# Two transformer blocks on one core: fillers that set the place of TensorE's operands in the on-chip memory

## The chip, the cores and the metric

One core of a Trainium2 chip. The metric is the device time of one execution in microseconds, the median of several runs.

## The reference

Two blocks of one layer each follow each other on 256 tokens of width 1024, with 16 learned tokens in front, all in fp32. The first mixes with two convolutions and then picks 16 of 16384 experts per token and head; the second has two kinds of attention, gates, and a feed-forward part.

```python
def first_block(x, meta_tokens, ...):
    ...
        proj = hn @ w_in[l]
    ...
        y = jnp.concatenate([rms_norm(y_sc, out_norm_g_sc[l]), rms_norm(y_cf, out_norm_g_cf[l])], axis=-1)
        h = h + y @ w_out[l]
        hn = rms_norm(h, norm_ffn_g[l])
        h = h + peer_layer(hn, peer_w_q[l], peer_sub_keys[l], peer_u[l], peer_v[l])
...
def second_block(x, meta, ...):
    ...
        proj = xn @ w_in[l]
        sb_q, sb_k, sb_v, df_q, df_k, df_v = jnp.split(proj, splits, axis=-1)
    ...
        y_sb = o_sb @ w_br_sb[l]
        y_df = o_df @ w_br_df[l]
        gates = jax.nn.sigmoid(xn @ w_gate[l] + b_gate[l]).reshape(B, L_pad, 2, D)
        merged = gates[:, :, 0] * y_sb + gates[:, :, 1] * y_df
        h = h + merged @ w_out[l]
        hn = rmsnorm(h, norm_ffn_g[l])
        h = h + (jax.nn.silu(hn @ w_ffn_gate[l]) * (hn @ w_ffn_up[l])) @ w_ffn_down[l]
    y = rmsnorm(h, norm_final_g)
    return y[:, N_META:N_META + S]
```

All 128 x 128 experts are computed for all tokens (`u`, then `v`), and the 16 chosen ones of each head get their gates.

## The kernel before, in words

**Units.** All large weights are cut into 454 units of 128 x 1024, listed in the order of use. SyncE's queue loads a unit into `raw` (five buffers, `load_to`); ScalarE copies it, rounded to fp32r, to `hi`, and VectorE writes the rest, `raw - hi`, to `lo` (three buffers each, `split_to`, lines 152 and 154). An activation is split in the same way. A product is three matmuls, hi x hi, hi x lo and lo x hi, summed in PSUM.

**Two kinds of matmul.** `mm_w` (lines 183 to 185) takes a unit as the stationary operand: for each of eight chunks of 128 columns it sends 256 or 272 columns of the activation through, 24 matmuls a unit. `mm_a` (lines 197 to 199) takes the activation as the stationary operand, 128 columns for each half of the tokens, and sends 512 columns of the unit through, 12 matmuls a unit. Each matmul loads its own 128 columns of weights; the profile calls those loads PEld, and they lie beside the matmul ahead.

**Stages, in order.** The projections of the first block from `xT` (`gg`, `ga`, `cg`, `xv`, `bg`); its output `wo` (`mm_a`, from `yhi`, `ylo`); queries `q` and 128 expert units `u` from `hThi`, `hTlo`; between these the routing, and in the second half of `u` the gate products `gp` (128-column fp32 matmuls in `pair`, taken from the list `pend` in the middle of a unit or ahead of one); 128 expert outputs `v` (`mm_a`, from `w_hi`, `w_lo`); six projections of the second block from `xT2` with the attention's own small matmuls between them (`stick`, `diff`); the gates `g`; the branches `ysb` and `ydf` from `osb` and `odf`; `o` (`mm_a`, from `mghi`, `mglo`); then `fg` and `fu` from `hThi`, `hTlo` and, in two halves within each `fg` unit, `fd` (`mm_a`, from `f_hi`, `f_lo`).

**Order.** TensorE's and SyncE's orders are as written; a scheduler orders the other engines. POOL's queue saves `h` (`hsave`, line 511), and loads it back with two gain rows towards the end of `v` (lines 835 to 840).

**Places.** A tile is a stretch of bytes that begins at the same place in each of the 128 partitions. A pool lays its tiles one behind the other, rounded up to 32 bytes, and pools stand on each other as a stack: 16384 bytes of scratch for the descriptors that POOL writes, then `const` (in it `hThi` and `hTlo`), `wraw`, `whi`, `wlo`, and the pools of the phases (`pc`, `pa`, `pb`, `pq`, `psb`, `pm`, `pf`). So every tile's place depends on all that stand ahead of it. In the attention, `sq` and `dq` (queries) and `sv` and `dv` (values) have two buffers each.

Of the kernel before, what the change touches and what calls it, by code (L numbers as in the profile page):

```python
# [9 lines left out]
F32 = mybir.dt.float32  # L10
# [9 lines left out]
P = 128  # L20
# [15 lines left out]
XN = 2  # L36
WARM = 9
SOON = 60

_VECS = [  # L40
    ("norm_mix_g", 8), ("norm_mix_g_2", 8), ("b_gate_2", 16),
# [11 lines left out]
def two_blocks(ctx, tc, x, feats, vecs, w_in, w_out, w_q, keys, u, v, final_g, meta2, w_in2, lams, w_gate,  # L53
               w_br_sb, w_br_df, w_out2, w_fg, w_fu, w_fd, final_g2, gains, out):
    nc = tc.nc
# [9 lines left out]
    def phase(name):  # L65
        st = ExitStack()
        pool = st.enter_context(tc.tile_pool(name=name, bufs=1, reuse_waits="tile"))
        return st, pool

    def mm_tile(name):  # L70
        return pmm.tile([P, 512], F32, tag="mm", name=name)
# [226 lines left out]
    s_c, pc = phase("pc")  # L298
# [160 lines left out]

    gf = gain_row(pc, 1, "gf", nc.sync)  # L460
    h = xt
    for br, (y, gname) in enumerate(((ysc, "out_norm_g_sc"), (cf, "out_norm_g_cf"))):
        ysq = pc.tile([P, 4, T], F32, tag=f"ysq{br}", name=f"ysq{br}")
        yhi = pc.tile([P, 4, T], F32R, tag=f"yhi{br}", name=f"yhi{br}")
        ylo = pc.tile([P, 4, T], F32R, tag=f"ylo{br}", name=f"ylo{br}")
        with first():
            for c in range(4):
                nc.scalar.activation(yhi[:, c, :], y[:, c, :], AF.Copy, scale=col(gname, c))
                nc.vector.scalar_tensor_tensor(ylo[:, c, :], y[:, c, :], col(gname, c), yhi[:, c, :].bitcast(F32),
                                               op0=ALU.mult, op1=ALU.subtract)  # L470
            for c in range(4):
                nc.scalar.activation(ysq[:, c, :], y[:, c, :], AF.Square)
            fold(ysq, 4, nc.gpsimd)
        acc = [mm_tile(f"wo{i}") for i in range(4)] if br == 0 else acc_tiles("wo1_")
        for c in range(4):
            if c < 2:
                mm_a(acc, [(yhi[:, c], ylo[:, c])], c == 0, False)
            elif c == 3:
                mm_a(acc, [(yhi[:, 2], ylo[:, 2]), (yhi[:, 3], ylo[:, 3])], False, True)
            if br == 0 and c == 0:  # L480
                with first():
                    norm_mean()
            if br == 0 and c == 1:
                with first():
                    norm_var()
            if c == 1:
                pss = at_tile(f"pss{br}") if br == 0 else mm_tile(f"pss{br}")
                for t in range(2):
                    nc.tensor.matmul(pss[:, t:t + 1], ysq[:, 0, t * P:(t + 1) * P], ones[:, :1], start=True, stop=True)
                rs = pc.tile([P, 2], F32, tag=f"rsb{br}", name=f"rsb{br}")  # L490
                nc.scalar.activation(rs, pss[:, :2], AF.Sqrt, bias=eps, scale=1.0 / 512)
                nc.vector.reciprocal(rs, rs)
        with first():
            for t in range(2):
                for b in range(2):
                    bs = slice(b * 512, (b + 1) * 512)
                    nc.vector.scalar_tensor_tensor(h[t][:, bs], acc[2 * t + b], rs[:, t:t + 1],
                                                   h[t][:, bs], op0=ALU.mult, op1=ALU.add)
# [29 lines left out]
    nc.sync.dma_start(lm, lams.broadcast_to((P, 4, 64)))  # L528
    lam = const.tile([P, 1], F32, tag="lam", name="lam")
    sg8 = const.tile([P, 1], F32, tag="sg8", name="sg8")  # L530

    vals_a = pr.tile([P, 2, NH, TOPK], F32, tag="vals", name="vals")
    pos_a = pr.tile([P, 2, NH, TOPK], U32, tag="pos", name="pos")
# [308 lines left out]
    s_q, pq = phase("pq")  # L842
# [5 lines left out]
    with first():  # L848
# [7 lines left out]
        for t in range(2):  # L856
            s1s.append(sq_sum(pb, hts[t], P, f"r2_{t}", junk))
    rsb = pq.tile([P, L], F32, tag="rsb", name="rsb")
    nc.gpsimd.memset(rsb[:, :NM], 1.0)

    def x2_norm():
# [87 lines left out]
    def stick(hd, q, k, vT):  # L949
        pz = at_tile(f"z{hd}")  # L950
        for kt in range(3):
            nc.tensor.matmul(pz[:, qcols(kt)], k[:, kt * P:(kt + 1) * P], q[:, Q0[kt]:], start=True, stop=True)
        z = psb.tile([P, NQ], F32, tag="z", name=f"zs{hd}", bufs=2)
        nc.vector.tensor_tensor(z, pz[:, :NQ], mneg, op=ALU.add)
        e = psb.tile([P, NQ], F32, tag="e", name=f"e{hd}", bufs=2)
        nc.scalar.activation(e, z, AF.Abs)
        nc.scalar.activation(e, e, AF.Exp, scale=-1.0)
        nc.scalar.activation(e, e, AF.Ln, bias=1.0)
        nc.vector.scalar_tensor_tensor(e, z, 0.0, e, op0=ALU.max, op1=ALU.add)
        yield  # L960
        vt = value(f"sv{hd}", "sv", vT)
        yield
        yield
        ps = at_tile(f"S{hd}")
        for kt in range(3):
            for j in range(kt, 3):
                nc.tensor.matmul(ps[:, qcols(kt, j)], tri if j == kt else ones, e[:, qcols(j)],
                                 start=(j == kt), stop=(j == 2))
        nc.vector.tensor_tensor(z, z, ps[:, :NQ], op=ALU.subtract)
        nc.scalar.activation(z, z, AF.Exp)  # L970
        yield
        yield
        po = at_tile(f"po{hd}")
        for kt in range(3):
            nc.tensor.matmul(po[:, Q0[kt]:T], vt[:, kt, :], z[:, qcols(kt)], start=(kt == 0), stop=(kt == 2))
        nc.scalar.activation(osb[0][:, hd, :], po[:, :T], AF.Copy)
        nc.vector.tensor_tensor(osb[1][:, hd, :], po[:, :T], osb[0][:, hd, :].bitcast(F32), op=ALU.subtract)
# [3 lines left out]
    def diff(hd, q, k, vT):  # L981
        slope = 2.0 ** (-(hd + 1))
        ws = []
        for t in range(2):
            kn = KN[t]
            nm = psb.tile([P, 2], F32, tag="nm", name=f"nm{hd}{t}", bufs=2)
            sm = psb.tile([P, 2], F32, tag="dsm", name=f"dsm{hd}{t}", bufs=2)
            pe = []
            for c in range(2):
                cs = slice(64 * c, 64 * c + 64)  # L990
                ps = at_tile(f"ds{hd}{t}{c}")
                nc.tensor.matmul(ps[:, :kn], q[cs, t * P:(t + 1) * P], k[cs, :kn], start=True, stop=True)
                s = psb.tile([P, kn], F32, tag=f"ds{t}{c}", name=f"dss{hd}{t}{c}", bufs=2)
                nc.vector.scalar_tensor_tensor(s, dist[t], -slope, ps[:, :kn], op0=ALU.mult, op1=ALU.add)
                nc.vector.tensor_reduce(nm[:, c:c + 1], s, axis=AX.X, op=ALU.max, negate=True)
                nc.scalar.activation(s, s, AF.Exp, bias=nm[:, c:c + 1], accum_out=sm[:, c:c + 1])
                pe.append(s)
            nc.vector.reciprocal(sm, sm)
            nc.vector.tensor_scalar(pe[1], pe[1], sm[:, 1:2], lam, op0=ALU.mult, op1=ALU.mult)
            w = padded[f"w{t}"][0]  # L1000
            nc.vector.scalar_tensor_tensor(w[:, :kn], pe[0], sm[:, 0:1], pe[1], op0=ALU.mult, op1=ALU.subtract)
            ws.append(w)
            if t == 0:
                yield
        vt = value(f"dv{hd}", "dv", vT)
        yield
        yield
        outs = []
        for t in range(2):
            nk = KW[t] // P  # L1010
            pw = at_tile(f"pw{hd}{t}")
            wT = psb.tile([P, 3, P], F32, tag="wT", name=f"wT{hd}{t}", bufs=2)
            for i in range(nk):
                nc.tensor.transpose(pw[:, i * P:(i + 1) * P], ws[t][:, i * P:(i + 1) * P], ident)
            nc.scalar.activation(wT[:, :nk, :], pw[:, :KW[t]].rearrange("p (a b) -> p a b", a=nk), AF.Copy)
            outs.append(wT)
        yield
        for t, wT in enumerate(outs):
            nk = KW[t] // P
            po = at_tile(f"dpo{hd}{t}")  # L1020
            for i in range(nk):
                nc.tensor.matmul(po[:, :P], wT[:, i, :], vt[:, i, :], start=(i == 0), stop=(i == nk - 1))
            nc.scalar.activation(od[t][:, hd, :], po[:, :P], AF.Copy)
# [25 lines left out]
                running.remove(g)  # L1049

    for hd in range(NH):
        q = feat(f"sq{hd}", hd, "sq", QS, float(P) ** -0.5) if hd != 1 else ahead
        if hd > 1:
            q = q()
            advance()
# [9 lines left out]
                cols = x2_norm()  # L1065
        vT = feat(f"svT{hd}", hd, "vT", FULL)
        if hd == 0:
            ahead = feat("sq1", 1, "sq", QS, float(P) ** -0.5)
            with first():
                across(pb, cols, rsb[:, QS], "rsb")  # L1070
            tc.keep_in_program_order(nc.scalar.preload_act_table_set("natural_log_exp_and_others"))
            q, k = q(), k()
# [4 lines left out]
            with queued([latest["hi"], latest["lo"]]):  # L1077
                small_parts()
    for hd in range(NH):
        q = feat(f"dq{hd}", hd, "dq", QS, 0.125)()  # L1080
        advance()
        k = feat(f"dk{hd}", hd, "k", FULL)()
        advance()
# [49 lines left out]
    nc.gpsimd.dma_start(gb2, final_g2.broadcast_to((P, D)))  # L1133
    acc = acc_tiles("fd")
    rsf = pf_.tile([P, T], F32, tag="rsf", name="rsf")
    prev = []

    def swish(m, pg, pu):
# [116 lines left out]
```

## Time and profile before

| | us |
|---|---|
| median of 3 runs (lowest, highest) | 1455.7 (1454.81, 1459.09) |
| the profiled execution | 1458.83 |
| its span, first to last instruction | 1456.8 |
| TensorE busy with matmuls | 1437.5 |
| VectorE, ScalarE, POOL busy | 1049.4, 741.1, 14.5 |
| TensorE's share of the chain that ended last | 92% |

The span lies within the profiled execution's own time. A line of the profile names the engine, the line of the kernel, the operation, output and inputs; PE is TensorE, DVE VectorE, ACT ScalarE. A matmul's record begins when it starts, and its end is modelled: records overlap, and the distance from start to start tells how fast they follow each other.

### The profile page before, as it was taken

Reading aid. Unit: us, or ns where it says so; the run is one execution under the profiler, and the core shown is the slowest. Engines: PE = TensorE matmul, PEld = TensorE weight load, DVE = VectorE, ACT = ScalarE, POOL = GpSimd, SP = SyncE. Lnnn points to the kernel's source line nnn. Section 1 sums busy time; section 2 is a strip of 40 time slices with the busy share of each in tenths; the row PEclk is TensorE's granted clock in tenths of the full one; section 3 lists DMA queues with packets and bytes.
Section 4 is the critical chain, followed back from the end, with each engine's and each line's share of the span. In section 5 each row is a group of like instructions: output and inputs, shape, how many; then the busy total and the mean of one; then the engine's idle time right before and its main releaser. Section 6 shows DMA issues by size and latency. Waiting matters only on the chain.

```text
span 1456.8 us, 25628 instructions
## 1 busy us (share of the span) xinstructions
PE 1437.5 (99%) x10114; PEld 1339.5 (92%) x10114; DVE 1049.4 (72%) x1887; ACT 741.1 (51%) x1236; POOL 14.5 (1%) x35
## 2 busy tenths in 40 slices
PE   8999999999999999999999999999999999999998
PEld 8988999999999999888888888899999999899997
DVE  8997789885889999655555565665577766766666
ACT  7555544544444444544444544564455764544444
POOL 0010000000000000000000000100000000000000
PEclk9999999999999999999999999999999999999999
DMA  7525565666444444566666676554344466555563
GB/s 242 198 73 186 194 186 174 192 198 194 145 138 138 145 146 137 181 191 198 190 192 197 191 247 197 175 172 127 121 130 125 137 178 186 172 179 184 188 191 100
DMA packets 69816, 248.96 MB, mean 171 GB/s; under 512 B 7744, under 2 KB 9152, under 8 KB 69696
## 3 DMA queue, kind: packets, MB, share of 16 engines
q1 hardware_dynamic: 68256, 242.61, 53.4%
q0 software_dynamic: 1152, 4.19, 0.8%
q8 instruction: 79, 1.29, 0.4%
q10 hardware_dynamic: 288, 0.52, 0.1%
q14 instruction: 41, 0.34, 0.1%
HBM read 245.20 MB, written 2.10 MB: 170 GB/s over the span
## 4 chain that ended last, share of the span: by engine, by line
PE 92%; DVE 6%; issue 1%; ACT 0%; DMA 0%; SPq 0%; DVEq 0%; ACTq 0%
PE v L197 8%; PE v L199 8%; PE v L198 8%; PE u L185 7%; PE u L183 7%; PE u L184 7%; PE gp L712 4%; DVE lo L154 2%; PE fg L184 1%; PE fg L185 1%; PE fu L185 1%; PE fu L183 1%; PE fu L184 1%; PE fg L183 1%; PE fd L199 1%; PE fd L198 1%
## 5 line engine op out<-in xcount | busy, mean ns | idle before, releaser
L154 DVE TENSOR_TENSOR lo<-raw,hi 128x1024 fp32r<-128x1024 f32 x453 | 551.4, 1222 | 233.2 <-ACT hi L152 231.4
L152 ACT ACTIVATE hi<-raw 128x1024 fp32r<-128x1024 f32 x453 | 476.3, 1057 | 406.8 <-PE u L184 98.2
L183 PE MATMUL u<-hThi,hi 128*128 128x256 f32 x1024 | 292.6, 286 | 0.0
L185 PE MATMUL u<-hThi,lo 128*128 128x256 f32 x1024 | 285.0, 278 | 0.9 <-DVE lo L154 0.6
L184 PE MATMUL u<-hTlo,hi 128*128 128x256 f32 x1024 | 284.5, 278 | 0.0
L198 PE MATMUL v<-lo,w_hi 128*128 128x512 f32 x512 | 199.3, 389 | 0.0
L199 PE MATMUL v<-hi,w_lo 128*128 128x512 f32 x512 | 199.3, 389 | 0.0
L197 PE MATMUL v<-hi,w_hi 128*128 128x512 f32 x512 | 199.2, 389 | 0.0
L185 PEld LDWEIGHTS u<-hThi,lo 128*128 128x128 f32 x1024 | 192.4, 188 | 2.0 <-DVE lo L154 1.8
L184 PEld LDWEIGHTS u<-hTlo,hi 128*128 128x128 f32 x1024 | 193.5, 189 | 0.0
L183 PEld LDWEIGHTS u<-hThi,hi 128*128 128x128 f32 x1024 | 192.7, 188 | 0.0
L198 PEld LDWEIGHTS v<-lo,w_hi 128*128 128x128 f32 x512 | 96.1, 188 | 20.2 <-DVE lo L154 0.2
L199 PEld LDWEIGHTS v<-hi,w_lo 128*128 128x128 f32 x512 | 96.1, 188 | 20.0
L197 PEld LDWEIGHTS v<-hi,w_hi 128*128 128x128 f32 x512 | 96.1, 188 | 19.7
L712 PE MATMUL gp<-ga,gb 128*128 128x128 f32 x512 | 69.9, 274 | 0.0
L806 ACT ACTIVATE w_hi<-ewa 128x512 fp32r<-128x512 f32 x48 | 30.3, 632 | 65.9 <-PE v L198 65.9
L712 PEld LDWEIGHTS gp<-ga,gb 128*128 128x128 f32 x512 | 63.6, 191 | 0.0
L808 DVE TENSOR_TENSOR w_lo<-ewa,w_hi 128x512 fp32r<-128x512 f32 x48 | 33.2, 693 | 38.6 <-ACT w_hi L806 38.6
L697 DVE TENSOR_TENSOR ga<-o,o 128x512 f32<-128x512 f32 x64 | 44.0, 687 | 19.0 <-PE gp L712 18.5
L184 PE MATMUL fg<-hTlo,hi 128*128 128x256 f32 x176 | 49.6, 282 | 0.5 <-DVE hTlo L245 0.5
L183 PE MATMUL fg<-hThi,hi 128*128 128x256 f32 x176 | 49.5, 282 | 0.3 <-ACT hThi L244 0.3
L183 PE MATMUL fu<-hThi,hi 128*128 128x256 f32 x176 | 49.6, 282 | 0.0
(409 smaller groups left out, 2963.1 us busy)
## 6 DMA issues: line engine op xcount, KB each, us to landing
raw<-in_u_dram SPq DMA_DIRECT2D x128, 512.0 KB, 3.6
raw<-in_v_dram SPq DMA_DIRECT2D x128, 512.0 KB, 3.6
raw<-in_w_in_dram SPq DMA_DIRECT2D x67, 512.0 KB, 3.6
raw<-in_w_fg_dram SPq DMA_DIRECT2D x22, 512.0 KB, 4.1
raw<-in_w_fu_dram SPq DMA_DIRECT2D x22, 512.0 KB, 3.5
raw<-in_w_fd_dram SPq DMA_DIRECT2D x22, 512.0 KB, 4.4
raw<-in_w_out_dram SPq DMA_DIRECT2D x16, 512.0 KB, 3.6
raw<-in_w_q_dram SPq DMA_DIRECT2D x16, 512.0 KB, 4.3
```

The source lines that it names most:

```text
L152: latest["hi"] = nc.scalar.activation(hi, loaded[i], AF.Copy)
L154: latest["lo"] = nc.vector.tensor_tensor(lo, loaded[i], hi.bitcast(F32), op=ALU.subtract)
L183: nc.tensor.matmul(ps, hi[:, ks], ahi[:, k, cols], start=(k == 0), stop=False)
L184: nc.tensor.matmul(ps, hi[:, ks], alo[:, k, cols], start=False, stop=False)
L185: nc.tensor.matmul(ps, lo[:, ks], ahi[:, k, cols], start=False, stop=(k == KC - 1))
L197: nc.tensor.matmul(ps, ahi[:, ts], hi[:, bs], start=first and n == 0, stop=False)
L198: nc.tensor.matmul(ps, ahi[:, ts], lo[:, bs], start=False, stop=False)
L199: nc.tensor.matmul(ps, alo[:, ts], hi[:, bs], start=False, stop=end)
L697: nc.vector.tensor_tensor(a.rearrange("p t (h l) -> p t h l", h=8), o8[:, tl, :].unsqueeze(3).broadcast_to((P, 4, 8, TOPK)), o16[:, tl, :] ...
L712: nc.tensor.matmul(p3[:, :, i], b[:, i, :], a[:, i, :], start=True, stop=True)
L806: nc.scalar.activation(hi, a, AF.Copy)
L808: nc.vector.tensor_tensor(lo, a, hi.bitcast(F32), op=ALU.subtract)
```

## The change

`fill` takes a tile that nobody writes or reads, so that what is laid out behind it stands further on. There are four: `const_end` (448 bytes) behind the tiles of `const`, `pc_end` (704) ahead of `ysq`, `yhi`, `ylo`, `pq_end` (640) ahead of `osb`, `odf`, `gate` and the pools above, and `pf_end` (704) ahead of the tiles of `swish`. The two small tiles `rsb0` and `rsb1` move from `pc` to `const` (64 bytes, ahead of `hThi`). The scratch is 8192 bytes instead of 16384. `sq` and `dq` share the two buffers `q`, `sv` and `dv` the two buffers `vt`.

No instruction is added or taken away, and on each engine they stand in the order of before; the waits of TensorE and VectorE are the same too. What differs is where tiles stand. The table gives the places in bytes modulo 1024. The weight tiles `hi` and `lo` begin at 480 before and at 992 after; a chunk of 128 columns is 512 bytes, so chunks begin at that place and 512 from it in turn.

| stage | activation | before | after | before, less the place of `hi` | after |
|---|---|---|---|---|---|
| `q`, `u`, `fg`, `fu` | `hThi`, `hTlo` | 928 | 992 | 448 (64 short of 512) | 0 |
| `ysb`, `ydf` | `osb`, `odf` | 864 | 992 | 384 | 0 |
| `v` | `w_hi`, `w_lo` | 480 | 992 | 0 | 0 |
| `wo` | `yhi`, `ylo` | 800, then 832 | 992 | 320, then 352 | 0 |
| `o` | `mghi`, `mglo` | 864 | 992 | 384 | 0 |
| `fd` | `f_hi`, `f_lo` | 800 | 992 | 320 | 0 |
| first projections | `xThi`; `xTlo` | 992; 480 | 480; 992 | 512; 0 | 512; 0 |
| second projections, `g` | `xT2hi`; `xT2lo` | 800; 288 | 288; 800 | 320; 832 | 320; 832 |

A chunk of `xT` or `xT2` is 272 columns, 1088 bytes, so that these begin 64 bytes further on with each chunk; a chunk of the other activations of `mm_w` is 1024 bytes.

```diff
+FY, FQ, FF = 704, 640, 704
...
+    def fill(pool, n, name):
+        pool.tile([P, n // 4], F32, tag=name, name=name)
...
     gf = gain_row(pc, 1, "gf", nc.sync)
     h = xt
+    fill(pc, FY, "pc_end")
...
-                rs = pc.tile([P, 2], F32, tag=f"rsb{br}", name=f"rsb{br}")
+                rs = const.tile([P, 2], F32, tag=f"rsb{br}", name=f"rsb{br}")
...
     sg8 = const.tile([P, 1], F32, tag="sg8", name="sg8")
+    fill(const, 448, "const_end")
...
     rsb = pq.tile([P, L], F32, tag="rsb", name="rsb")
+    fill(pq, FQ, "pq_end")
...
-        vt = value(f"sv{hd}", "sv", vT)
+        vt = value(f"sv{hd}", "vt", vT)
...
-        vt = value(f"dv{hd}", "dv", vT)
+        vt = value(f"dv{hd}", "vt", vT)
...
-        q = feat(f"sq{hd}", hd, "sq", QS, float(P) ** -0.5) if hd != 1 else ahead
+        q = feat(f"sq{hd}", hd, "q", QS, float(P) ** -0.5) if hd != 1 else ahead
...
-            ahead = feat("sq1", 1, "sq", QS, float(P) ** -0.5)
+            ahead = feat("sq1", 1, "q", QS, float(P) ** -0.5)
...
-        q = feat(f"dq{hd}", hd, "dq", QS, 0.125)()
+        q = feat(f"dq{hd}", hd, "q", QS, 0.125)()
...
     rsf = pf_.tile([P, T], F32, tag="rsf", name="rsf")
+    fill(pf_, FF, "pf_end")
...
-    nc = _bacc.Bacc("TRN2", target_bir_lowering=False, num_devices=1)
+    nc = _bacc.Bacc("TRN2", target_bir_lowering=False, num_devices=1, dynamic_dma_scratch_size=8192)
```

## Rows read from the trace of the kernel before

**Rows 1.** The page: busy time by engine; granted TensorE clock in 40 slices.
```profile
PE 1437.5 (99%) x10114; PEld 1339.5 (92%) x10114; DVE 1049.4 (72%) x1887; ACT 741.1 (51%) x1236; POOL 14.5 (1%) x35
...
PEclk9999999999999999999999999999999999999999
```

**Rows 2.** Waits of TensorE: who, releaser: us in total, times, longest.
```profile
PE tr_h L241 <- DVE hn L508: 2.7, 3, 1.7
```

**Rows 3.** Groups by line: shape, count, busy us, mean ns of one, idle.
```profile
L199 PE MATMUL v<-hi,w_lo 128*128 128x512 f32 x512 | 199.3, 389 | 0.0
...
L185 PE MATMUL g<-xT2hi,lo 128*128 128x256 f32 x128 | 35.9, 281 | 0.0
...
L199 PE MATMUL fd<-hi,f_lo 128*128 128x512 f32 x88 | 34.9, 396 | 0.0
L198 PE MATMUL fd<-lo,f_hi 128*128 128x512 f32 x88 | 34.8, 396 | 0.0
L197 PE MATMUL fd<-hi,f_hi 128*128 128x512 f32 x88 | 34.7, 394 | 0.0
```

**Rows 4.** Line L184 by output: duration in ns, least/median/greatest.
```profile
L184 PE MATMUL u<-hTlo,hi x1024: 275/276/286, 131.7 to 591.3; 128*128 128x256 f32 x171
...
L184 PE MATMUL fg<-hTlo,hi x176: 280/281/384, 1263.6 to 1438.5; 128*128 128x256 f32 x176
...
L184 PE MATMUL q<-hTlo,hi x128: 275/276/416, 124.5 to 274.3; 128*128 128x256 f32 x128
```

**Rows 5.** Line L199 by output, the same columns.
```profile
L199 PE MATMUL v<-hi,w_lo x512: 388/389/398, 592.0 to 939.6; 128*128 128x512 f32 x171
...
L199 PE MATMUL wo<-hi,ylo x32: 390/394/500, 89.4 to 117.8; 128*128 128x512 f32 x32
...
L199 PE MATMUL o<-hi,mglo x32: 390/393/404, 1223.6 to 1259.4; 128*128 128x512 f32 x32
```

**Rows 6.** Timeline in `v` (start us, us, instruction), first and last of 178.
```profile
599.69 0.39 PE L197 MATMUL v<-hi,w_hi 128*128 128x512 f32 x1
...
639.81 0.39 PE L197 MATMUL v<-hi,w_hi 128*128 128x512 f32 x1
```

**Rows 7.** Timeline in `u`, first and last of 188.
```profile
325.73 0.28 PE L184 MATMUL u<-hTlo,hi 128*128 128x256 f32 x1
...
346.93 0.28 PE L185 MATMUL u<-hThi,lo 128*128 128x256 f32 x1
```

**Rows 8.** Timeline from `fg` through `fu` into `fg`, ends of 45.
```profile
1336.26 0.28 PE L183 MATMUL fg<-hThi,hi 128*128 128x256 f32 x1
...
1341.44 0.28 PE L185 MATMUL fg<-hThi,lo 128*128 128x256 f32 x1
```

**Rows 9.** Timeline in `ysb`, first and last of 179.
```profile
1192.77 0.28 PE L185 MATMUL ysb<-osbhi,lo 128*128 128x256 f32 x1
...
1213.89 0.28 PE L183 MATMUL ysb<-osbhi,hi 128*128 128x256 f32 x1
```

**Rows 10.** Groups, then busy (PE, PEld, DVE, ACT, POOL), 367 to 590 us.
```profile
L184 PE MATMUL u<-hTlo,hi 128*128 128x256 f32 x477 | 133.2, 279 | 0.0
L185 PE MATMUL u<-hThi,lo 128*128 128x256 f32 x477 | 133.0, 279 | 0.0
...
367.00:590.00 223.00, 223.00 (x1943) 223.00 (x1942) 200.68 (x362) 100.76 (x271) 0.00 (x0) 1.00 0.46 141
```

**Rows 11.** POOL's timeline; chain near 940 us; DMA issues (us to landing).
```profile
844.45 1.05 POOL L840 DMA_DIRECT2D ht<-hsave  x2
...
940.70 1.20 DVE x L853 x2
...
ht<-hsave POOLq DMA_DIRECT2D x2, 512.0 KB, 9.5
```

**Rows 12.** Timeline at the start of `v`: first and sixth matmul.
```profile
591.51 0.40 PE L197 MATMUL v<-hi,w_hi 128*128 128x512 f32 x1
...
592.67 0.39 PE L199 MATMUL v<-hi,w_lo 128*128 128x512 f32 x1
```

## The prediction

> **What bounds the kernel now.** The page comes first: TensorE is busy for 1437.5 of 1456.8 us, and its granted clock stands at nine tenths or more in every slice [rows 1]. The waits of TensorE come next: the costliest single cause is 2.7 us over three waits [rows 2]. So the time is a sum of matmul steps, and I look for steps that are longer than others of the same width.
>
> The groups of TensorE instructions by line show them. A 512-column matmul takes 389 ns in the `v` stage, but 394 to 396 ns in `fd`; `g`, with 256 columns, takes 281 ns [rows 3]. The durations of one line by stage show the same for 256 columns: the median is 276 ns in `u`, 281 ns in `fg` with a shortest of 280 ns [rows 4]. For 512 columns the medians of line L199 are 389 ns in `v`, 394 in `wo` and 393 in `o` [rows 5].
>
> The ends of these records are modelled, so I take the distance from start to start, which is what the sum needs. In the timeline of `v` 177 steps take 40.12 us: 226.7 ns each [rows 6]. In quiet `u` 187 steps take 21.20 us: 113.4 ns, half of that [rows 7]. Across `fg` and `fu` 44 steps take 5.18 us: 117.7 ns [rows 8]. In `ysb` 178 steps take 21.12 us: 118.7 ns [rows 9]. A record is about 163 ns longer than its step in each of these stages, so a difference of durations [rows 3 to 5] can be read as a difference of steps.
>
> Now the places (the table ahead) beside the steps, for 512 columns: `v`, whose `w_hi` and `w_lo` stand where the weight tiles do, has the short step; `wo`, `o` and `fd`, which stand elsewhere, are 4 to 7 ns longer. For 256 columns: `u` stands 64 bytes short of the weight tiles and has the short step in quiet stretches, `fg` stands at the same two places and has the long one, `ysb` at a third and has the longest. So the place matters, but for 256 columns it doesn't settle the rhythm alone.
>
> **The change part by part.** It adds no instruction, and all keep their order; the sum is made of steps alone. The reference step is the short one: 226.7 ns and 113.4 ns.
>
> - `fg`, `fu`: 2 x 22 units x 24 = 1056 matmuls, each 117.7 - 113.4 = 4.3 ns shorter: 4.5 us.
> - `ysb`, `ydf`: 16 x 24 = 384, each 118.7 - 113.4 = 5.3 ns: 2.0 us.
> - `fd`: 88 of each of three lines, 7 + 7 + 5 ns over 389 [rows 3]: 1.7 us.
> - `wo`: 96, 394 - 389 = 5 ns by the medians [rows 5]: 0.5 us. `o`: 96, 393 - 389 = 4 ns: 0.4 us.
> - `u` among the gate products (367 to 590 us): the lines L184 and L185 take 279 ns on the mean, 3 over the 276 of quiet stretches [rows 4, 10]; 2 x 477 x 3 ns = 2.9 us. The third line, L183, mostly holds the restart behind each `gp`, which stays; I count nothing of it.
> - `q` and `u` elsewhere have the short step already (medians of 276 ns) [rows 4]: 0. So has `v`, which is equal in place before and after: 0.
> - The projections that read `xT` and `xT2`: one chunk is 1088 bytes, so the place moves by 64 from chunk to chunk and takes all eight values, before and after. I take 0. Half a nanosecond on their 2016 matmuls (480 and 1536) would be 1 us either way; I keep that for the range.
> - Buffers shared by `sq` with `dq` and by `sv` with `dv`, `rsb` in another pool: a wait could arise where the first two heads of the second attention overwrite what the last heads of the first have read; the order and the waits of TensorE and VectorE are the same as before, so 0.
> - Half the scratch of the POOL queue's descriptors: the only cluster of its transfers is that of `gb`, `gain` and twice `ht`, the last issued from 844.45 us, and VectorE's first use of `ht` is over at 940.70 us, when line 853 begins [rows 11]. A stall of the queue has some 95 us of cover; without that cover it would cost about one landing, 9.5 us [rows 11], which I don't add.
>
> Full sum: 4.5 + 2.0 + 1.7 + 0.5 + 0.4 + 2.9 = 12.0 us. Not all of it comes. After a switch the short rhythm has to settle: on entering `v` five steps take 591.51 to 592.67 us, 232 ns each [rows 12], and only then 227 [rows 6]; that is about 26 ns a switch. `fd` comes in some 40 pieces between `fg` matmuls (20 units, two halves): 40 x 26 ns = 1.0 us. `gp` breaks into `u` once or twice in each unit, which leaves some two thirds of that term: 1.8 instead of 2.9 us. VectorE is at 200.7 of 223 us in that stretch [rows 10], which also speaks for less. So 12.0 - 1.0 - 1.1 = 9.9 us.
>
> The profiled execution took 1458.8 us (span 1456.8 and 2.0 around it), 3.1 above the median of 1455.7. 1458.8 - 9.9 = 1448.9; from the median **1445.8 us**.
>
> The one unknown price is the step of 256 columns at an equal place, which no row has. Its nearest rows: `v` at the equal place, half of 226.7 = 113.4; `u`, 64 bytes away, 113.4 or, among `gp`, more; `ysb`, 118.7. I take 113.4, since the equal place is that of `v`, and in `v` it held for some 350 us: of its 512 matmuls on L199 the median is 389 ns and the longest 398 [rows 5]. A shorter step is excluded by the same row: `v` keeps 2 x 113.4 over 177 steps with the weight load to spare.
>
> **The rule that speaks against it.** The Trainium skill, page "TensorE: Matmul & The Clock Gate", section "Part 2: What happens when you issue a matmul", says that the array has two independent read ports to the on-chip memory, so that loading the next weights takes nothing from the running matmul. By it the places of the operands are of no account and the sum is 0. The rows on `v`, `o` and `fd`, same width and same clock with steps 4 to 7 ns apart, don't agree with it unless something else sets them apart.
>
> **Rivals.**
>
> *The place is not the cause (1455.7 us).* `fd` and `o` differ from `v` also in standing in short pieces between other matmuls, and `fg` differs from quiet `u` at identical places. If history makes the rhythm, nothing moves. Against it: `wo` runs 12 and more 512-column matmuls in a row and stays at the long step, while `v` is at the short one after five. 9 in 100.
>
> *Only the 512-column stages gain (1453.1 us).* 1.7 + 0.5 + 0.4 = 2.6 us, if the 256-column rhythm goes on as it is. 10 in 100.
>
> *The equal place is a bad one for 256 columns (slower).* There the next load starts with every 256 columns, and only `u`'s place is known to allow the short step. If the equal place gives `ysb`'s 118.7 ns, the quiet `q` and `u` matmuls (384 + 3072 - 1431 = 2025) lose 5.3 ns each, 10.7 us; `u` among `gp`, which has 3 of these 5.3 ns already, loses 1431 x 2.3 = 3.3 us; `fg` and `fu` lose 1.0 ns, 1.1 us; less 2.6: +12.5, 1468.2 us. With `fg`'s 117.7 ns it is 8.7 + 1.9 (1431 x 1.3 ns), less 0.4 (`ysb`, `ydf`, 384 x 1.0) and 2.6: +7.6, 1463.3 us. The point from which it decides: with `fg`, `fu` where they are, the 2.6 us are lost as soon as three tenths of the quiet matmuls take the long step. For it: `g`, whose chunks pass through all the places, has 281 ns on the mean [rows 3], so one place among them at 276 can't be seen there. Against it: the half step of `v`. 15 in 100.
>
> *The 256-column stages flip between the two rhythms.* Half of the gain of `fg`, `fu`, `ysb`, `ydf`, none in `u`: 2.6 + 3.3 = 5.9 us, 1449.8 us. 6 in 100.
>
> **How the numbers follow.** The forecast has 60 in 100, and reaches from the full sum with the 1 us of the projections and half a microsecond of scatter (1455.7 - 13.5, about 1442) to a gain of 7 (1449). The range takes in the flipping rhythm, the 512-column case and no change with 1 us of scatter: 1442 to 1457; outside lie the bad place and a little below. 0.3%, 4.4 us, is about what a measurement of this kernel can tell from no change. Faster by more: 60 + 6 = 0.66. Within: 10 + 9 = 0.19. Slower: 0.15.
>
> **What would show it.** In the groups by line: `fg`, `fu`, `ysb`, `ydf` at 276 to 277 ns instead of 281 to 282; `fd` and `o` near 389 to 391; `u`'s L184 at a mean of 277 with the median still 276; `v` at 389 and `q` at 276 as before; TensorE's waits as small as now. The medians of `u` and `q` decide: 281 there is the bad place. `fd` at 389 with `fg` at 281 is the 512-column case; all as before, and the place was not the cause.

## The result and the profile after

The change makes the kernel slower: 1470.4 us (1469.33 to 1471.64) against 1456.6 us (1454.81 to 1459.09), a ratio of 1.0084 with an interval from 1.0068 to 1.0101, so 13.8 us more. It was forecast at 1445.8 us, within 1442 to 1457.

The page of the changed kernel, engines and granted clock, answers to [rows 1]: TensorE still bounds it, at the full clock, and is busy longer.

```profile
PE 1449.4 (99%) x10114; PEld 1354.8 (92%) x10114; DVE 1048.7 (71%) x1887; ACT 742.3 (51%) x1236; POOL 15.5 (1%) x35
...
PEclk9999999999999999999999999999999999999999
```

The second line of `mm_w` by output (it is L188 now, L184 before): duration in ns, least, median and greatest. It answers to [rows 4].

```profile
L188 PE MATMUL u<-hTlo,hi x1024: 280/283/284, 128.6 to 601.7; 128*128 128x256 f32 x171
L188 PE MATMUL fg<-hTlo,hi x176: 280/283/389, 1272.5 to 1449.0; 128*128 128x256 f32 x176
...
L188 PE MATMUL q<-hTlo,hi x128: 278/283/386, 122.8 to 275.7; 128*128 128x256 f32 x128
...
L188 PE MATMUL ysb<-osblo,hi x64: 283/283/284, 1200.7 to 1223.4; 128*128 128x256 f32 x64
```

Every stage of 256 columns that now stands at the equal place has 283 ns, where `u` and `q` had 276 and `fg` 281. The third line of `mm_a` (L203 now, L199 before), which answers to [rows 5]:

```profile
L203 PE MATMUL v<-hi,w_lo x512: 389/389/392, 602.4 to 949.9; 128*128 128x512 f32 x171
...
L203 PE MATMUL wo<-hi,ylo x32: 387/390/504, 89.0 to 116.6; 128*128 128x512 f32 x32
...
L203 PE MATMUL o<-hi,mglo x32: 389/389/393, 1232.8 to 1268.3; 128*128 128x512 f32 x32
```

With 512 columns the equal place did what was forecast: `wo` came from 394 to 390 ns and `o` from 393 to 389. So one change of place has two signs, and the width decides which.

The timeline in quiet `u` of the changed kernel, first and last of 178 matmuls, beside [rows 7]:

```profile
319.75 0.28 PE L188 MATMUL u<-hTlo,hi 128*128 128x256 f32 x1
...
340.99 0.28 PE L188 MATMUL u<-hTlo,hi 128*128 128x256 f32 x1
```

177 steps take 21.24 us: 120.0 ns each instead of 113.4. Busy TensorE, matmuls, granted clock, DMA share and GB/s in two stretches, first before, then after:

```profile
117.00:130.00 13.00, 10.25 (x57) 0.74 0.45 165
125.00:365.00 240.00, 238.51 (x2066) 0.99 0.61 187
```

```profile
117.00:130.00 13.00, 9.80 (x77) 1.00 0.48 171
125.00:365.00 240.00, 240.00 (x2007) 1.00 0.59 183
```

The same 240 us hold 59 matmuls fewer, although the profile before lost time there that the one after did not lose: its granted clock was 0.74 on the mean from 117 to 130 us, and 17 steps from 124.5 us on took some 100 ns more each, about double, as at 1.2 instead of 2.4 GHz. TensorE had waited for `hn` just before [rows 2]; after the change it waited as well, and in this execution the clock stayed. Nothing shows that the change kept it up: over all executions the mean granted clock is 0.994 to 0.999 before and 0.997 to 1.000 after, and the profile after is the one at 1.000.

Summed over all steps of a stage in the two traces (from the start of one record to the start of the next, less the shortest step, 113.3 or 226.7 ns; steps over 15 ns longer, with something else between, are left out), in us:

| stage | steps | before | after | difference | forecast |
|---|---|---|---|---|---|
| `q` and the first 64 units of `u` | 1920 | 0.6 | 12.6 | +12.0 | 0 |
| the other 64 units of `u` | 1536 | 3.7 | 9.2 | +5.5 | -1.8 |
| `fg`, `fu` | 1056 | 4.8 | 6.7 | +1.9 | -4.5 |
| `ysb`, `ydf` | 384 | 2.0 | 2.5 | +0.5 | -2.0 |
| `fd` | 264 | 1.7 | 1.2 | -0.5 | -0.7 |
| `wo`, `o` | 192 | 1.1 | 0.4 | -0.7 | -0.9 |
| `v` | 1536 | 0.0 | 0.0 | 0 | 0 |

That is 18.7 us. The spans of the two profiles (1456.8 and 1467.2 us) differ by 10.4. Of the 8.3 us between, 3.3 are the time that the profile before spent at a lower clock (those 17 steps, and 16 from 943.8 us on), and 3.8 lie in longer steps of `q` and the first half of `u` that the table leaves out. In the profile before, ten matmuls between 223 and 318 us start 55 or 56 ns after VectorE has written the `lo` that they read; the steps into and out of them take 4.0 us above 113.3 ns each. In the profile after one of the ten is left, 0.1 us. The longest, before:

```profile
250.68 1.21 DVE L154 TENSOR_TENSOR lo<-raw,hi 128x1024 fp32r<-128x1024 f32 x1
...
251.28 0.28 PE L184 MATMUL q<-hTlo,hi 128*128 128x256 f32 x1
...
251.94 0.38 PE L185 MATMUL q<-hThi,lo 128*128 128x256 f32 x1 [0.38 <-DVE lo L154]
```

The view of TensorE's waits, which [rows 2] show for the costliest alone, has four of the ten, since the modelled end of the record ahead covers the others (us in total, times, longest):

```profile
PE u L185 <- DVE lo L154: 0.6, 2, 0.3
PE q L185 <- DVE lo L154: 0.5, 2, 0.4
```

So while VectorE also does the routing, TensorE catches up with it at the short step and waits; at the long one it hardly does. That gave back 3.8 of the 18.7 us.

### The profile page after: what moved, and what is told of

It reads as the page before. It is cut to its first block, busy times and chain, and to the rows that moved or that the text cites. A ratio compares the mean times of both kernels' runs of the same rounds, so it can differ in the third digit from the quotient of the medians.

```text
span 1467.2 us, 25628 instructions
## 1 busy us (share of the span) xinstructions
PE 1449.4 (99%) x10114; PEld 1354.8 (92%) x10114; DVE 1048.7 (71%) x1887; ACT 742.3 (51%) x1236; POOL 15.5 (1%) x35
## 4 chain that ended last, share of the span: by engine, by line
PE 96%; DVE 2%; ACT 1%; DMA 0%; issue 0%; SPq 0%; ACTq 0%; DVEq 0%
PE u L188 8%; PE u L187 8%; PE u L189 8%; PE v L203 8%; PE v L202 8%; PE v L201 8%; PE gp L718 4%; PE fg L188 1%; PE fu L187 1%; PE fu L188 1%; PE fu L189 1%; PE fg L189 1%; PE fg L187 1%; PE fd L201 1%; PE fd L202 1%; PE fd L203 1%
## 5 line engine op out<-in xcount | busy, mean ns | idle before, releaser
L156 ACT ACTIVATE hi<-raw 128x1024 fp32r<-128x1024 f32 x453 | 476.0, 1056 | 415.7 <-PE u L188 108.1
L187 PE MATMUL u<-hThi,hi 128*128 128x256 f32 x1024 | 297.5, 291 | 0.0
L189 PE MATMUL u<-hThi,lo 128*128 128x256 f32 x1024 | 289.6, 283 | 0.0
L188 PE MATMUL u<-hTlo,hi 128*128 128x256 f32 x1024 | 289.5, 283 | 0.0
L203 PE MATMUL v<-hi,w_lo 128*128 128x512 f32 x512 | 199.2, 389 | 0.0
L188 PEld LDWEIGHTS u<-hTlo,hi 128*128 128x128 f32 x1024 | 196.4, 192 | 0.0
L187 PEld LDWEIGHTS u<-hThi,hi 128*128 128x128 f32 x1024 | 196.1, 192 | 0.0
L189 PEld LDWEIGHTS u<-hThi,lo 128*128 128x128 f32 x1024 | 195.9, 191 | 0.0
L203 PEld LDWEIGHTS v<-hi,w_lo 128*128 128x128 f32 x512 | 96.1, 188 | 19.8
L188 PE MATMUL fg<-hTlo,hi 128*128 128x256 f32 x176 | 49.9, 284 | 0.3 <-DVE hTlo L249 0.3
```

Source lines behind the costliest of these rows:

```text
L156: latest["hi"] = nc.scalar.activation(hi, loaded[i], AF.Copy)
L187: nc.tensor.matmul(ps, hi[:, ks], ahi[:, k, cols], start=(k == 0), stop=False)
L188: nc.tensor.matmul(ps, hi[:, ks], alo[:, k, cols], start=False, stop=False)
L189: nc.tensor.matmul(ps, lo[:, ks], ahi[:, k, cols], start=False, stop=(k == KC - 1))
L203: nc.tensor.matmul(ps, alo[:, ts], hi[:, bs], start=False, stop=end)
```

## Experiments

All edits are to the changed kernel, unless said otherwise. "Place" is that of the activation less that of the weight tiles `hi` and `lo`, modulo 512. The row shown is the second line of `mm_w` (L188, or L184 in the kernel before), with the columns as above. Its median alone does not give the step (at 64 and 192 a step of 117.8 ns shows as 279 to 281), so steps are given from start to start, in ns over 113.3 or 226.7. Such a step is a mean over a unit or a stretch: single steps can alternate about it (4 and 9 ns over, in `v` at 64 below). A rhythm is a pattern of steps that goes on from matmul to matmul.

### 1. The queries alone, back at 448 and alone at 0

```diff
-    fill(const, 448, "const_end")
```

> The changed kernel without the filler const_end: hThi and hTlo (q, u, fg, fu) stand 448 bytes on from the weight tiles again, as before the change; all other activations stay at the equal place, and the shared buffers and the halved scratch stay. Theory (the equal place lengthens a 256-column step from 113.4 to 120 ns and shortens a 512-column one): the medians of q and u go back to 276 ns, and the time to 1455 us (1456.6, less about 1.2 for wo, o and fd, plus 0.5 for ysb and ydf). Rival (the shared buffers, the scratch or the absolute place of the weight tiles cost the time): q and u stay at 283 ns and the time at 1470 us.

1455.5 us against 1456.2 before: ratio 0.9999 (0.9986 to 1.0013). The whole loss is gone with one filler.

```profile
L188 PE MATMUL u<-hTlo,hi x1024: 276/281/283, 130.1 to 594.6; 128*128 128x256 f32 x171
...
L188 PE MATMUL q<-hTlo,hi x128: 276/281/416, 123.4 to 275.6; 128*128 128x256 f32 x128
```

So neither the shared buffers nor the smaller scratch nor the other fillers cost anything that can be measured. But the medians were a miss: they are 281, not 276. At the very distance where the first profile had the short step, quiet `u` now has 117.8 ns; 180 steps from 319.73 us take 21.20 us. No operand's own place settles the step: `hThi` stands at 992 here as in the changed kernel, and the weight tiles stand at 480 before and at 992 after, the same modulo 512. It is the distance between the two that counts. `fd`, with `fg` and `fu` away from the equal place, came down to 389 or 390 ns on all three lines; in the changed kernel two of them stay at 395.

```diff
-FY, FQ, FF = 704, 640, 704
+FY, FQ, FF = 0, 0, 0
...
-    fill(pc, FY, "pc_end")
...
-    fill(pq, FQ, "pq_end")
...
-    fill(pf_, FF, "pf_end")
```

> The changed kernel with the filler const_end alone: only q, u, fg, fu stand at the equal place; wo, o, fd, ysb and ydf stand away from it again. Theory: q and u at 283 ns, fd and o back at 393 to 396 ns, ysb at 281: the time of the change plus 1 us, 1471 us. Rival (the fillers pc_end, pq_end, pf_end and what lies behind them cost the time): 1456 us with u at 276 ns.

1472.5 us, ratio 1.0111 (1.0092 to 1.0130). `u` has 283 ns, and `ysb` is back at 281; both as the theory has it.

```profile
L188 PE MATMUL u<-hTlo,hi x1024: 278/283/287, 129.6 to 602.7; 128*128 128x256 f32 x171
...
L188 PE MATMUL ysb<-osblo,hi x64: 279/281/285, 1201.7 to 1224.2; 128*128 128x256 f32 x64
```

### 2. Other places for every stage

```diff
-FY, FQ, FF = 704, 640, 704
+FY, FQ, FF = 832, 704, 1024
...
-    fill(const, 448, "const_end")
+    fill(const, 192, "const_end")
...
+    fill(pv_, 64, "pv_end")
```

> Other places for every stage at once. Activation less weights, modulo 512: q, u, fg, fu 256; ysb, ydf 64; wo 128; v 64; o 64; fd 320. If only the equal place is bad for 256 columns, q, u, fg, fu and ysb have 276 ns. If 448 is the one good place, they have 281 to 283 ns. For v at 64 the theory that the place sets the 512-column step expects 393 to 396 ns instead of 389 (4 to 7 ns on 1536 steps, 6 to 11 us more); the rival, that short pieces between other matmuls made fd, o and wo long, expects v to stay at 389. The time: 1455 with all 256-column stages short and v at 389, 1481 with all of them long.

1482.2 us, ratio 1.0180 (1.0158 to 1.0201).

```profile
L188 PE MATMUL u<-hTlo,hi x1024: 280/283/283, 129.0 to 602.0; 128*128 128x256 f32 x171
...
L188 PE MATMUL ysb<-osblo,hi x64: 279/279/279, 1211.4 to 1233.7; 128*128 128x256 f32 x64
```

```profile
L201 PE MATMUL v<-hi,w_hi 128*128 128x512 f32 x512 | 202.5, 396 | 0.0
```

256 is as bad as 0 (6.7 ns). `v`, in the same long row of matmuls as ever, goes from 389 to 396 ns: 6.7 ns a step, 10.2 us in all. The 512-column step follows the place, and the pieces in which `fd` and `o` stand are not what made them long (in the first experiment `fd` has 389 or 390 ns in the same pieces).

```diff
-FY, FQ, FF = 704, 640, 704
+FY, FQ, FF = 960, 768, 1088
...
-    fill(const, 448, "const_end")
+    fill(const, 320, "const_end")
...
+    fill(pv_, 192, "pv_end")
```

> Other places again, activation less weights modulo 512: q, u, fg, fu 128; ysb, ydf 128; wo 256; v 192; o 128; fd 384. The same two theories for 256 columns: 276 ns in q, u, fg and ysb if only the equal place is bad, 281 to 283 ns if 448 is the one good place. v at 192: 393 to 396 ns if the place sets the 512-column step, 389 if it does not. The time: 1455 to 1481 us, as for the other places.

1470.7 us, ratio 1.0103 (1.0082 to 1.0125). At 128, units of `u` have 5.3 or 6.7 ns; `ysb` has 5.3. So "only the equal place is bad" fell. `v` at 192 has 2.2 ns, less than expected; `o` and `fd`, at 128 and 384, have 5.3.

```profile
L188 PE MATMUL u<-hTlo,hi x1024: 274/282/287, 128.7 to 600.2; 128*128 128x256 f32 x171
```

### 3. Finer places, and 448 shifted by 256

The next three hold `wo`, `v`, `o` and `fd` at the equal place, with a filler ahead of `mg`. Fillers `const_end`, `FQ`, ahead of `mg`: 480, 1088, 64; then 416, 736, 416; then 256, 960, 192.

> q, u, fg, fu 32 bytes short of the equal place (480 modulo 512), ysb and ydf at 448; wo, v, o, fd at the equal place. Seen so far for 256 columns, as ns over 113.3: at 0 and 256 always 6.7; at 128 and 384 either 5.3 or 6.7; at 64 4.5; at 448 either 0 or 4.5, from unit to unit. Theory (two rhythms, and the finer the remainder of the distance, the smaller the excess of both): at 480, an odd multiple of 32, both rhythms of q, u, fg, fu lie at or under those of 448, some 0 to 2 ns, 276 to 278 ns in the groups by line, and the time is 1445 to 1449 us. Rival (distances closer to the equal place come closer to its step): 282 ns and 1468 us. ysb and ydf at 448 have 0 or 4.5.

> q, u, fg, fu 32 bytes behind the equal place, ysb and ydf at 96; wo, v, o, fd at the equal place. Theory of the remainder: as at 480, 276 to 278 ns and 1445 to 1449 us. Rival (closeness): 282 ns, 1468 us. A third case, that the sign counts (the weight load runs ahead of or behind the columns): 480 short and 32 long, or the other way round.

> q, u, fg, fu at 192, ysb and ydf at 320, both odd multiples of 64; wo, v, o, fd at the equal place. Theory of the remainder: as at 448, units with 0 and units with 4.5 ns over 113.3, switching at disturbances, so 1450 to 1460 us. Rival (448 alone allows the short rhythm): all units near 5 ns, 281 ns in the groups by line, 1463 us.

1463.8 us at 480 (ratio 1.0071, 1.0053 to 1.0089), 1461.3 at 32 (1.0050, 1.0033 to 1.0067), 1456.1 at 192 (1.0014, 1.0003 to 1.0025). The rows of `u` in this order:

```profile
L188 PE MATMUL u<-hTlo,hi x1024: 277/281/285, 130.8 to 599.6; 128*128 128x256 f32 x171
```

```profile
L188 PE MATMUL u<-hTlo,hi x1024: 277/280/282, 130.7 to 595.1; 128*128 128x256 f32 x171
```

```profile
L188 PE MATMUL u<-hTlo,hi x1024: 276/276/286, 132.4 to 593.6; 128*128 128x256 f32 x171
```

The theory of the finer remainder fell: quiet units have 5.0 ns at 480 and 3.3 at 32, and no unit is near 0. At 192 it held: of the first 64 units 35 have 0.0 and 16 have 4.4 or 4.5; in the rest, with a mean between, a restart stands in the unit or the step changes within it. `ysb` at 448 (beside 480) and at 320 (beside 192) has 4.5.

### 4. The kernel before once more

No edit.

> The kernel before, unchanged, for a second profile. Theory (at 448 the steps have two rhythms, 113.3 and 117.8 ns, and what lies ahead of a stretch decides which one holds): other stretches of q and u than in the first profile have the long rhythm, and the time lies within the 1451 to 1461 us seen, earlier or later by 4.5 ns for each step that differs. Rival (the place and the instruction order settle the rhythm): the same units are long and short as in the first profile, u 276 ns below 365 us.

1457.9 us. The rows of L184:

```profile
L184 PE MATMUL u<-hTlo,hi x1024: 276/281/286, 132.0 to 595.3; 128*128 128x256 f32 x171
L184 PE MATMUL fg<-hTlo,hi x176: 276/276/388, 1266.4 to 1437.6; 128*128 128x256 f32 x176
...
L184 PE MATMUL q<-hTlo,hi x128: 276/281/415, 124.5 to 276.8; 128*128 128x256 f32 x128
```

The same program at the same places: `u` and `q` have a median of 281 where they had 276 [rows 4], and `fg` has 276 where it had 281. From `fg` through `fu` 44 steps take 5.00 us, 113.6 ns each, where [rows 8] have 117.7; the timeline, first and last of 45:

```profile
1345.84 0.28 PE L183 MATMUL fg<-hThi,hi 128*128 128x256 f32 x1
...
1350.84 0.28 PE L185 MATMUL fg<-hThi,lo 128*128 128x256 f32 x1
```

Summed as in the table of the result, `q` and the first 64 units take 5.3 us more than in the first profile, `fg` and `fu` 3.7 less. So at 448 place and program do not settle the step of the quiet stretches. It has two rhythms, and one holds until a disturbance: among the gate products it changes at nearly every `gp`. There the two profiles agree: of 65 stretches of eight or more steps 64 have the same rhythm in both, and the excess of that half is 3.7 and 3.8 us. The rhythms are a part of the scatter of the kernel before, whose runs in all comparisons lie between 1451.0 and 1462.2 us. The clock is another: runs with a mean granted clock of 0.999 have 1453.6 us on the mean (1451.0 to 1458.0), those with 0.995 or 0.996 have 1457.0. How much of the rest the rhythms make was not measured run by run.

### 5. Attempts at a place that holds the short step

In the first two, `hi` and `lo` of an activation stand apart, by fillers between their tiles (here `hT` of the first; `osb` and `odf` likewise):

```diff
+    hThi = const.tile([P, KC, T], F32R, tag="hThi", name="hThi")
+    fill(const, 256, "hT_gap")
+    hT = (hThi, const.tile([P, KC, T], F32R, tag="hTlo", name="hTlo"))
```

> An attempt at a better version: hi and lo of the activation at different odd multiples of 64 from the weight tiles: hThi 448 and hTlo 192; osbhi 448 and osblo 64; odfhi 448 and odflo 320; wo, v, o, fd at the equal place. Theory (two rhythms at all odd multiples of 64): q, u, fg, fu have 113.3 or 117.8 ns, 1452 to 1460 us. Hope: where hi and lo differ, the long rhythm cannot hold, and all units have 113.3: 1445 us. Rival: mixing two places brings a third, longer rhythm, 281 to 283 ns, 1465 us.

> The same attempt with hThi 64 and hTlo 448; osbhi 192 and osblo 448; odfhi 320 and odflo 448. The same three cases: 1452 to 1460 us with both rhythms, 1445 us if the long one is gone, 1465 us if a third one comes.

1455.5 us (ratio 1.0003, 0.9991 to 1.0015): both rhythms, 28 of the first 64 units with 0.0 and 29 with 4.4 or 4.5. And 1462.4 us (1.0048, 1.0030 to 1.0065): nearly all units 4.4 to 4.7, and none short. The hope failed in both.

```diff
-    fill(const, 448, "const_end")
...
-    xT2 = (pq.tile([P, KC, L], F32R, tag="xT2hi", name="xT2hi"), pq.tile([P, KC, L], F32R, tag="xT2lo", name="xT2lo"))
+    fill(pq, 320, "xT2_front")
+    xT2 = tuple(pq.tile([P, KC, 384], F32R, tag=n, name=n)[:, :, :L] for n in ("xT2hi", "xT2lo"))
...
+    fill(pm, 192, "pm_front")
```

> A version that should beat both if the short rhythm comes: as the first experiment (q, u, fg, fu at 448; wo, v, o, fd at the equal place), ysb and ydf at 320, and the chunks of xT2 1536 bytes apart instead of 1088, so that their place no longer walks: sq, dq and g (256 columns, 768 steps) stand at 192 in all chunks, the 272-column steps at 128. Theory: sq, dq, g have 0 or 4.5 ns over 113.3, where the walking place gave 3.8 to 4.7 on the mean, so 276 or 281 ns in the groups by line and a gain of 3.5 us at best; the 272-column steps have no constant place so far, and may gain or lose 3 us on 768. The time: 1450 to 1458 us. Rival (where the chunk begins does not matter there): g stays at 281 and the 272-column steps at 289 ns, and the time is that of the first experiment, 1455 us.

1454.8 us against 1454.6: ratio 1.0002 (0.9991 to 1.0013). `g` at a constant 192 gained 0.9 us in this profile (line L188 at 279 ns on the mean instead of 281), `sq` and `dq` nothing, and the 272-column steps lost 0.3 us together. It beats neither the first experiment nor the kernel before. By chance its profile has the short step in nearly all of `q` and the first half of `u` (0.3 us over, against 8.0 in that of the first experiment), and there the waits for `lo` are 4.2 us, against 1.3: about 3 of those 8 us are lost again to VectorE.

The last three move `q`, `u`, `fg`, `fu` once more: to 64 (`const_end` 384), to 416 (32), and, with tiles used from 16 bytes on, `hThi` to 432 and `hTlo` to 464 (480).

> q, u, fg, fu 64 bytes behind the equal place instead of 64 short of it, ysb and ydf at 192; wo, v, o, fd at the equal place. Theory of the remainder: 64 is an odd multiple of 64 as 192 and 448 are, so units with 0 and units with 4.5 ns over 113.3, 1452 to 1460 us. Rival (the side counts; ysb at 64 and the kernel with hThi at 64 showed 4.5 alone): no unit of q or u below 4 ns, 281 ns throughout, 1463 us.

> q, u, fg, fu at 416 (160 modulo 256), ysb and ydf at 480; wo, v, o, fd at the equal place. Seen so far in quiet q and u, ns over 113.3, by the distance modulo 256: 0 6.7, 32 3.3, 64 4.5, 96 6.5, 128 5.3 or 6.7, 192 0 or 4.5, 224 5.0. Theory (192 alone has the short rhythm): 3 to 6 ns in all units, 279 to 282 ns, 1459 to 1465 us. Rival (160 lies between 128 and 192, and the short rhythm holds there without a long one): 276 ns and 1446 us.

> hThi at 432 and hTlo at 464, 16 bytes on each side of 448 (their tiles are longer by 32 bytes and begin to be used 16 bytes in); ysb, ydf, wo, v, o, fd at the equal place. Theory (a place has to be a multiple of 64 for the short rhythm): 3 to 6 ns over 113.3 in all units, 279 to 282 ns, 1459 to 1465 us. Rival (16 bytes do not count): 0 and 4.5 ns from unit to unit as at 448, 1452 to 1460 us.

1462.3 us at 64 (ratio 1.0056, 1.0037 to 1.0076), 1465.1 at 416 (1.0059, 1.0040 to 1.0077), 1467.2 at 432 and 464 (1.0078, 1.0059 to 1.0097). The rows of `u`, in this order:

```profile
L188 PE MATMUL u<-hTlo,hi x1024: 276/280/280, 128.4 to 595.4; 128*128 128x256 f32 x171
```

```profile
L188 PE MATMUL u<-hTlo,hi x1024: 277/281/284, 128.5 to 596.4; 128*128 128x256 f32 x171
```

```profile
L188 PE MATMUL u<-hTlo,hi x1024: 279/282/285, 130.8 to 600.8; 128*128 128x256 f32 x171
```

At 64 nearly all units have 4.4 or 4.5, as the rival had it, but not quite all: from 244.4 us on 22 steps and from 251.0 us on 33 steps are short. At 416 quiet units have 4.0 or 5.3, at 432 and 464 5.3: 16 bytes on either side of 448 take the short step away. What the runs show together, in ns over the shortest step:

| place modulo 256 | 256 columns | 512 columns |
|---|---|---|
| 0 | 6.7 | 0 (`v`) |
| 32 | 3.3 | not tried |
| 64 | 4.5 (two short stretches at 0) | 6.7 (`v`) |
| 96 | 6.7 (`ysb`) | 7.4 (second half of `wo`, before) |
| 128 | 5.3 or 6.7 | 5.3 (`o`, `fd`) |
| 160 | 4.0 or 5.3 | not tried |
| 192 | 0 or 4.5 | 2.2 (`v`) |
| 224 | 5.0 | not tried |

Places 256 bytes apart behave alike wherever both were seen: 0 and 256, 128 and 384, 64 and 320, 192 and 448.

## Why the prediction was wrong

**What bounds the kernel** was right in the main: a sum of TensorE steps. That waits are of no account was not quite so: the view of waits gives those for `lo` in `q` and `u` as 1.1 us, but by the starts of the matmuls they and the steps behind them took 4.0 us, and 3.8 of these went with the short step. **The place as a cause** was right too, for both widths, and "the place is not the cause" fell with the first experiment. The Trainium skill, page "TensorE: Matmul & The Clock Gate", section "Part 2: What happens when you issue a matmul", says that two independent read ports let the next weights load without taking anything from the running matmul. What the prediction drew from it, that places are of no account, does not hold here: with the order of the row unchanged, `v` went from 389 to 396 ns by place alone. By what the place acts no run shows, so the ports themselves are not refuted.

**The 512-column terms** had the right sign. For `wo` and `o` 0.9 us were forecast and 0.7 came. For `fd` 1.7 were forecast, less 1.0 for settling, and 0.5 came; with `fg` and `fu` back at 448 it gained 1.6. The settling cost depends on the rhythm of the neighbours and was no constant of 26 ns.

**The step that failed** is the one unknown price: "I take 113.4, since the equal place is that of `v`". A price was carried from 512 columns to 256. The equal place has 120.0 ns there, above both ends of the bounds (113.4 and `ysb`'s 118.7): a bound taken from other places was no bound. All terms of 256 columns took the other sign by it, and 2.6 us of gain in the others at most could not pay for it. The rival "the equal place is a bad one for 256 columns" had the mechanism, the sign, and with 1468.2 us nearly the size. That it was only 2.2 us short is luck in part: with the measured 120.0 ns its sum is 1474.6 us, 4.2 too long, about what came back with the waits for `lo`, which it does not know. Its share of 15 in 100 was too small: the argument against it was half a step of `v`, while `fg`, `ysb` and `g` all had the long step [rows 3, 4, 9], which spoke for a rule of their own at 256 columns.

**A second step** was wrong without deciding the sign: that quiet `u` and `q` "have the short step already" as if it belonged to their place. It was one of two rhythms at 448, as the second profile of the kernel before showed. The prediction saw that `fg` has the long step at `u`'s place and said that the place does not settle the rhythm alone, but summed as if it did. By the two profiles of the kernel before, `q` and the first half of `u` differ by 5.3 us in their steps (by 4.0 with waits and clock) between executions of one program, so the 1455.7 us that the sum started from comes out of a mixture of rhythms.

**Terms set to nothing** held, but for the waits for `lo`: no other wait grew by more than 0.5 us, and shared buffers, the moved `rsb` and the smaller scratch leave no trace in the first experiment. The projections from `xT` and `xT2` changed by some 0.1 us a stage at most.

What stays open: why a short step lasts at 192 modulo 256 alone, what in a disturbance chooses the rhythm, and by what the place acts. No run found a place that holds the short step, or a version that beats the kernel before by more than the intervals.

## What to carry to other kernels

When TensorE is busy all the time, compare its steps from start to start between stages of the same width, and take the place of both operands modulo 256 bytes as one candidate for a difference. Don't carry the price of a place from one shape to another: a filler is one line, so try each width alone before all are moved together. And before a good step is put down to anything in the program, look at a second profile of the same program: here 4.5 ns a step came and went by themselves. And ask what a shorter step would run into: here some of it was lost again to VectorE.

## What had not been expected of the hardware

The same two operands can follow each other in two stable rhythms, 113.3 or 117.8 ns for 256 columns, each held over hundreds of steps and changed at disturbances. The step depends on the distance of the operands, alike at places 256 bytes apart wherever both were seen, and with `hi` and `lo` 16 bytes off 448 no unit is short. The best place for 512 columns, 0, is among the worst for 256: 120.0 ns against 113.3, while 226.7 ns are kept there with 512.
